# A depthwise convolution taken from VectorE to GpSimd (one half) and TensorE (the other half)

## The chip, the cores and the metric

The kernel runs on one core of a Trainium2 chip. The metric is the device time of one execution in microseconds (us). The kernel before takes 3819.85 us, the median of three runs from 3814.09 to 3823.12 us. The engines are named as in the profile: PE (TensorE, matrix products), PEld (its weight loads), DVE (VectorE), ACT (ScalarE), POOL (GpSimd) and SP (SyncE, which issues most of the transfers).

## What is computed

The whole network is a first block (attention, a state-space layer, a feed-forward layer with retrieved experts) and a second block of two layers. Each layer of the second block is feed-forward, mixer, feed-forward, on 512 tokens of width 1024. The mixer projects the tokens once, gives the parts to four sub-mixers, and projects the joined result back:

```
z = rmsnorm(x, mix_norm) @ w_in
(aq, ak, av, iq, ik, iw, bq, bk, bv, bg, br, cu, dcq, dckv, dkpe) = split(z)
y_a = dsa_mixer(aq, ak, av, iq, ik, iw, ...)     # attention over keys chosen by an index score
y_b = gla_mixer(bq, bk, bv, bg, br, ...)         # gated linear attention
y_c = conv_mixer(cu, c_dw_w, c_dw_b, c_norm)
y_d = mla_mixer(dcq, dckv, dkpe, ...)            # attention from latents
x = x + concatenate([y_a, y_b, y_c, y_d]) @ w_out

def conv_mixer(u, w_dw, b_dw, g_norm):
    a, gate = split(u, 2)
    h = a * sigmoid(gate)
    h = depthwise_conv(h, w_dw, padding=[(30, 0)]) + b_dw   # 31 taps, each of 256 channels by itself
    return silu(rmsnorm(h, g_norm))
```

The change concerns the depthwise convolution alone: 256 channels, 31 taps, 512 tokens. With channels on the 128 partitions these are two chunks of 128 x 512 numbers. Each of the 31 taps adds the input, shifted by the tap's number of tokens and multiplied by one number per channel.

## The kernel before

The feature dimension lies on the partitions and the 512 tokens along the free dimension. A projection block `proj(b)` makes 128 output features. Its weight (128x1024, `wr`) comes in by DMA. It is split into a high part `wh` by ACT (L1009) and a low part `wl` = `wr` - `wh` (L1010), on POOL for most of the mixer's blocks and on DVE for a few. 24 products of 128x512 follow on PE (L195 to L197: high by high, high by low, low by high, for 8 chunks). `wr`, `wh` and `wl` have two buffers each, so a weight is prepared at most two blocks ahead. The products accumulate in PSUM, and DVE evacuates them with the norm factor (L1066).

The mixer is a list of named steps (`ORDER`) that is issued in that order. A list scheduler with priorities then fixes one static order of instructions per engine. Each engine runs its own list in order, and a wait at the head of a list holds all that is behind it. The steps in the neighbourhood of the change are `hp` (the four projection blocks of the convolution, gated into the tile `hp`, `conv_in`), `ik`, `t3` and `iq` (blocks for the index score), `index` (the index score: PE L1234, ACT L1236, then DVE L1239/L1241), `lat` (three blocks for the latent attention, lat0 to lat2 below), and `conv`. `index` runs interleaved with `lat`. `conv` is 62 instructions on DVE: per chunk one TENSOR_SCALAR that also adds the bias (L1539) and 30 SCALAR_TENSOR_TENSOR that multiply and add (L1541). Far behind them stand `mla` (the latent attention), `qkn`, `rg` and `silu` (gates; L1120 also works on the convolution's result), and the four pieces `dsa0` to `dsa3`, before the output projection `wo`.

Of the kernel before, what the change touches and what calls it, by code (L numbers as in the profile page):

```python
# [9 lines left out]
F32 = mybir.dt.float32  # L10
# [3 lines left out]
AF = mybir.ActivationFunctionType  # L14
OP = mybir.AluOpType
# [4 lines left out]
P = 128  # L20
D = 1024
NCH = 8
T = 512
# [789 lines left out]
TAGS = {"x": 16, "ml": 12, "ds": 7, "sm": 4, "sd": 4, "gl": 10, "r": 2, "t3": 1, "rg": 2, "cv": 2, "rs": 1}  # L813
F_GRP = ((0, 8), (8, 15), (15, 22))
SWAP = np.r_[16:32, 0:16]
ORDER = "hp ik t3 iq exp index lat mla_in conv bqk v3 gla_in v2 v0 gla mla0 v1 mla1 mla3 qk mla2 qkn conv_norm topk2 rg silu topk1 y4 y2 topk3 y6 dsa0 dsa3 dsa1 dsa2".split()
WOP = ((0, 4, 2), (4, 8, 2))
YORD = (4, 5, 2, 3, 6, 7, 0, 1)

# [86 lines left out]
class Block2:  # L906
# [143 lines left out]
    def mixer(self, l, x):  # L1050
        net, nc, w, p = self.net, self.nc, self.w, self.p
        V = nc.vector
        first = {b: self.lw(self.A["w2"][l, b], 1024) for b in (13, 15)}
        xh, xl, rx = self.scaled(x, "mix")

        def proj(b):
            wh, wl = (a.rearrange("p (c m) -> p c m", c=NCH)
                      for a in first.pop(b, None) or self.lw(self.A["w2"][l, b], 1024, nc.vector if b in (14, 16) else nc.gpsimd))
            ps = net.ps("pa", "win")
            for c in range(NCH):  # L1060
                net.mm3(ps, (wh[:, c], wl[:, c]), (xh[c], xl[c]), c == 0, c == NCH - 1)
            return ps

        def keep(b, tag):
            t = self.mt(tag)
            V.tensor_mul(t, proj(b), rx)  # L1066
            return t

        def rsc():
            return self.mt("r")  # L1070

        def glsc():
            return self.mt("gl")
# [26 lines left out]
        def gla():  # L1100
            with net.banks("pd", "gla", glsc):
                v["gla"] = self.gla(v["glain"], *v["bqk"], vt)

        def mla(j):
            if "ya" not in v:
                v["ya"] = p.tile([P, 2, T + 30], F32, tag="hp", name=net.nm("ya"))[:, :, :T]
            with net.banks("pb", "mla"):
                self.mla(j, v["mla"], v["ya"])

        def qkn():  # L1110
            with net.banks("pc", "qkn", rsc):
                v["rq"] = self.qk_norm(v["qk"])

        def conv_norm():
            with net.banks("pd", "convn", rsc):
                self.conv_norm(v["acc"])

        def silu():
            for t in v["rg"] + v["acc"]:
                self.tc.keep_in_program_order(nc.scalar.activation(t, t, AF.Silu))  # L1120
            self.exp_set()

        def ysplit(c):
            for m in range(2):
                k = c + m
                yh[k], yl[k] = self.mt("x", F32R), self.mt("x", F32R)
                if c == 4:
                    src = v["acc"][m]
                elif c == 2:
                    src = v["gla"][m]  # L1130
                    V.tensor_mul(src, src, v["rg"][m])
                else:
                    src = v["ya"][:, m]
                net.split(src, yh[k], yl[k])

        def dsa(j):
            for c in range(2):
                if yh[c] is None:
                    yh[c], yl[c] = self.mt("x", F32R), self.mt("x", F32R)
            with net.banks(("pb", "pc")[j % 2], "dsa"):  # L1140
                self.dsa(j, v["masks"][j], v["qk"], v["rq"], vt, yh, yl, ("sm", "sd")[j % 2])

        steps = {
            "hp": lambda: v.update(hp=self.conv_in(proj, rx)),
            "exp": self.exp_set,
            "t3": lambda: v.update(t3=keep(3, "t3")),
            "iq": lambda: v.update(iq=[keep(0, "ds"), keep(1, "ds")]),
            "ik": lambda: v.update(ik=keep(2, "ds")),
            "index": index,
            "lat": lambda: v.update(lat=[keep(b, "ml") for b in (10, 11, 12)]),  # L1150
            "mla_in": mla_in,
            "bqk": lambda: v.update(bqk=[keep(8, "gl"), keep(9, "gl")]),
            "gla_in": gla_in,
            "conv": lambda: v.update(acc=self.conv(l, v["hp"])),
            "qk": lambda: v.update(qk=[keep(b, "ds") for b in (4, 5, 6, 7)]),
            "qkn": qkn,
            "gla": gla,
            "rg": lambda: v.update(rg=[keep(17, "rg"), keep(18, "rg")]),
            "conv_norm": conv_norm,
            "silu": silu,  # L1160
        }
        for j in range(4):
            steps[f"v{j}"] = lambda j=j: values(j)
            steps[f"mla{j}"] = lambda j=j: mla(j)
            steps[f"dsa{j}"] = lambda j=j: dsa(j)
            steps[f"topk{j}"] = lambda j=j: self.topk(v["masks"][j])
        for c in (2, 4, 6):
            steps[f"y{c}"] = lambda c=c: ysplit(c)
        for s in ORDER:
            steps[s]()  # L1170

        for a, e, g in WOP:
            for m0 in range(0, NCH, g):
# [39 lines left out]
    def index(self, iq, ik, t3):  # L1213

        net, nc, w, p = self.net, self.nc, self.w, self.p
        V = nc.vector
        iw = w.tile([P, 4, 8], F32, tag="iw", name=net.nm("iw"))
        ps = net.ps()
        for i in range(4):
            nc.tensor.transpose(ps[:, i * 8:(i + 1) * 8], t3[32:40, i * P:(i + 1) * P], net.c("ident")[32:40, 32:40])  # L1220
# [2 lines left out]
        for j in (3, 2, 1):  # L1223
            n = (j + 1) * P
            ts = slice(j * P, n)
            acc = self.mt("ds")[:, :n]
            for h in range(8):
# [5 lines left out]
                ps = net.ps()  # L1233
# [158 lines left out]
    def mla(self, j, qkv, ya):  # L1392
# [6 lines left out]
        for h in range(4):  # L1399
# [3 lines left out]
            if j:  # L1403
                nc.scalar.activation(sm[h][:, :j * P], ps[:, :j * P], AF.Identity, scale=r)
            V.scalar_tensor_tensor(sm[h][:, ts], ps[:, ts], r, self.caus, op0=OP.mult, op1=OP.add)
        self.softmax_pv(sm, n, lambda k, h: kv[k][:, 256 + h * 64:256 + (h + 1) * 64],
                        lambda c, po: nc.scalar.activation(ya[:, c, ts], po, AF.Copy))

    def gla_in(self, l, bq, bk, t3):
        net, nc, w, p = self.net, self.nc, self.w, self.p  # L1410
# [105 lines left out]
            out.append(o)  # L1516
        return out

    def conv_in(self, proj, rx):
        net, nc, w, p = self.net, self.nc, self.w, self.p  # L1520
        hp = p.tile([P, 2, T + 30], F32, tag="hp", name=net.nm("hp"))
        nc.gpsimd.memset(hp[:, :, :30], 0.0)
        for m in range(2):
            pa, pg = proj(13 + m), proj(15 + m)
            sg = net.sc(w)
            nc.vector.tensor_mul(hp[:, m, 30:], pa, rx)
            nc.vector.tensor_mul(sg, pg, rx)
            nc.scalar.activation(sg, sg, AF.Sigmoid)
            nc.vector.tensor_mul(hp[:, m, 30:], hp[:, m, 30:], sg)
        return hp  # L1530

    def conv(self, l, hp):
        net, nc, w = self.net, self.nc, self.w
        V = nc.vector
        dw = w.tile([P, 2, 31], F32, tag="dw", name=net.nm("dw"), bufs=1)
        nc.scalar.dma_start(dw.rearrange("p a b -> p (a b)"), self.A["dw"][l])
        acc = self.mts("cv", 2, F32)
        for m, a in enumerate(acc):
            V.tensor_scalar(a, hp[:, m, 0:T], dw[:, m, 0:1], self.gv("cb", m), op0=OP.mult, op1=OP.add)  # L1539
            for k in range(1, 31):  # L1540
                V.scalar_tensor_tensor(a, hp[:, m, k:k + T], dw[:, m, k:k + 1], a, op0=OP.mult, op1=OP.add)  # L1541
        return acc

    def conv_norm(self, acc):
        net, w = self.net, self.w
# [393 lines left out]
```

## Time and profile before

| | |
|---|---|
| median of three runs | 3819.85 us |
| the profiled execution | 3817.53 us, of which its span is 3815.8 us |
| PE busy | 3638.3 us (95%), 17229 instructions |
| DVE busy | 2584.0 us (68%) |
| ACT busy | 1444.5 us (38%) |
| POOL busy | 1087.8 us (29%), 693 instructions |
| the mixer of layer 0 | about 2065 to 2372 us |
| the mixer of layer 1 | about 3130 to 3442 us |

The span is the part of an execution that the profile covers. Busy times are of one execution, over very unlike stages: the first block takes up to about 1690 us, the two layers of the second block the rest. In a row of the timeline the first number is the start in microseconds from the start of the span, the second the length from the first start to the last end of the instructions merged in the row, and in brackets stands how long the engine was idle before it and whose end released it. The two mixers are built alike and only one of them needs to be read closely.

### The profile page before, as it was taken

How to read it: one execution, taken by the hardware profiler on the slowest of the kernel's cores; microseconds unless marked ns; L12 is line 12 of the kernel's file. 1: busy time of each engine (PE TensorE's matmuls, PEld its weight loads, DVE VectorE, ACT ScalarE, POOL GpSimd, SP SyncE). 2: the span in 40 equal slices, each digit the busy share in tenths (PEclk: the TensorE clock that was granted, in tenths of full speed). 3: DMA queues.
4: the chain of work that ended last, by engine and by line, in shares of the span. 5: the costliest groups of instructions: out<-in, count | busy, mean ns of one | idle time of the engine just before them, and what ended most of it. 6: DMA issues, size and time to landing. Idle time of an engine off the chain costs nothing.

```text
span 3815.8 us, 46368 instructions
## 1 busy us (share of the span) xinstructions
PE 3638.3 (95%) x17229; PEld 2975.1 (78%) x17229; DVE 2584.0 (68%) x4684; ACT 1444.5 (38%) x2401; POOL 1087.8 (29%) x693
## 2 busy tenths in 40 slices
PE   7798989989999999989999899999999998999999
PEld 6656877878988988878887577788788875667887
DVE  8668988788888888844445987434444459874343
ACT  3253369623333333342223446322322234463222
POOL 4424767455555555530001222000100013210000
PEclk8899989999999999999999999999999999999999
DMA  4212224788888888832222111222222221112223
GB/s 118 77 39 98 75 99 178 270 305 304 285 312 293 300 293 293 301 102 94 94 97 91 53 45 56 94 94 94 94 94 93 95 91 61 45 47 92 94 94 99
DMA packets 182081, 529.89 MB, mean 139 GB/s; under 512 B 22112, under 2 KB 73888, under 8 KB 163680
## 3 DMA queue, kind: packets, MB, share of 16 engines
q1 hardware_dynamic: 157840, 389.36, 30.6%
q0 software_dynamic: 18944, 134.75, 9.6%
q10 hardware_dynamic: 5072, 2.81, 0.3%
q8 instruction: 136, 2.23, 0.2%
q14 instruction: 89, 0.73, 0.1%
HBM read 495.51 MB, written 30.18 MB: 138 GB/s over the span
## 4 chain that ended last, share of the span: by engine, by line
PE 69%; DVE 8%; ACT 3%; DMA 3%; issue 2%; POOL 1%; ACTq 0%; POOLq 0%; DVEq 0%
PE ps L195 13%; PE ps L197 13%; PE ps L196 13%; PE V L1815 11%; PE S L197 3%; PE S L196 3%; PE S L195 3%; DVE cv L1541 2%; PE G L1749 2%; ACT gst L1750 1%; PE win L195 1%; PE win L197 1%; PE win L196 1%; DVE ds L1241 1%; DMA vr<-in_uv_dram 1%
## 5 line engine op out<-in xcount | busy, mean ns | idle before, releaser
L1009 ACT ACTIVATE wh<-wr 128x1024 fp32r<-128x1024 f32 (+1 forms) x334 | 347.4, 1040 | 1056.5 <-PE ps L196 759.4
L197 PE MATMUL ps<-x,wl 128*128 128x512 f32 x1408 | 557.0, 396 | 0.0
L195 PE MATMUL ps<-x,wh 128*128 128x512 f32 x1408 | 556.7, 396 | 0.0
L196 PE MATMUL ps<-x,wh 128*128 128x512 f32 x1408 | 556.6, 395 | 0.0
L989 POOL TENSOR_TENSOR s<-s,s 128x512 f32<-128x512 f32 x42 | 66.7, 1588 | 1161.6 <-ACT s L987 1150.4
L1806 POOL TENSOR_TENSOR vl<-vr,vh 128x1024 fp32r<-128x1024 f32 x128 | 324.2, 2533 | 177.8 <-ACT vh L1805 168.0
L1010 DVE TENSOR_TENSOR wl<-wr,wh 128x1024 fp32r<-128x1024 f32 (+1 forms) x288 | 343.9, 1194 | 43.8 <-ACT wh L1009 37.1
L197 PE MATMUL S<-pxh,ul 128*128 128x384 f32 x1024 | 349.7, 341 | 7.6 <-POOL ul L1767 7.6
L195 PE MATMUL S<-pxh,uh 128*128 128x384 f32 x1024 | 349.3, 341 | 0.0
L196 PE MATMUL S<-pxl,uh 128*128 128x384 f32 x1024 | 348.4, 340 | 0.0
L195 PEld LDWEIGHTS ps<-x,wh 128*128 128x128 f32 x1408 | 265.8, 189 | 63.9 <-ACT ml L947 1.1
L197 PEld LDWEIGHTS ps<-x,wl 128*128 128x128 f32 x1408 | 265.7, 189 | 62.7 <-issue 0.7
L196 PEld LDWEIGHTS ps<-x,wh 128*128 128x128 f32 x1408 | 265.8, 189 | 62.2 <-issue 0.5
L1815 PE MATMUL V<-vl,ah 128*128 128x512 f32 x768 | 303.5, 395 | 9.7 <-POOL vl L1806 9.7
L1815 PE MATMUL V<-vh,ah 128*128 128x512 f32 x768 | 300.7, 392 | 5.0 <-ACT vh L1805 2.6
L1815 PE MATMUL V<-vh,al 128*128 128x512 f32 x768 | 304.1, 396 | 0.9 <-DVE al L181 0.8
L195 PE MATMUL ps<-ml,wh 128*128 128x512 f32 x704 | 277.8, 395 | 0.0
L197 PE MATMUL ps<-ml,wl 128*128 128x512 f32 x704 | 277.8, 395 | 0.0
L1035 DVE TENSOR_TENSOR s<-ps,rs 128x512 f32<-128x512 f32 x88 | 60.9, 692 | 304.7 <-PE ps L197 304.7
L1876 POOL DMA_INDIRECT rows<-in_uv_dram,gidx x128 | 189.7, 1482 | 256.6 <-DVE acc L1885 225.7
L1047 DVE SCALAR_TENSOR_TENSOR hT<-ps,hT 128x512 f32<-128x512 f32 x96 | 66.4, 692 | 268.5 <-PE ps L197 268.5
L1767 DVE TENSOR_TENSOR ul<-ur,uh 128x1024 fp32r<-128x1024 f32 x100 | 184.8, 1848 | 65.8 <-ACT uh L1765 64.6
(578 smaller groups left out, 7997.4 us busy)
## 6 DMA issues: line engine op xcount, KB each, us to landing
wr<-in_f_gu_dram SPq DMA_DIRECT2D x176, 512.0 KB
ur<-in_ut_dram SPq DMA_DIRECT2D x128, 512.0 KB
vr<-in_uv_dram SPq DMA_DIRECT2D x128, 512.0 KB
wr<-in_f_dn_dram SPq DMA_DIRECT2D x64, 448.0 KB
gates<-gst SPq DMA_DIRECT2D x12, 2048.0 KB
gt<-gates SPq DMA_DIRECT2D x32, 768.0 KB
wr<-in_w_dram SPq DMA_DIRECT2D x46, 512.0 KB
wr<-in_f_dn_dram SPq DMA_DIRECT2D x32, 512.0 KB
```

The source lines that it names most:

```text
L195: mm(out, wh, xh, start=start, stop=False)
L196: mm(out, wh, xl, start=False, stop=False)
L197: mm(out, wl, xh, start=False, stop=stop)
L989: nc.gpsimd.tensor_tensor(sq, acc, sq, op=OP.add)
L1009: nc.scalar.activation(hi, raw, AF.Copy)
L1010: (eng or nc.vector).tensor_tensor(lo, raw, hi.bitcast(F32), op=OP.subtract)
L1541: V.scalar_tensor_tensor(a, hp[:, m, k:k + T], dw[:, m, k:k + 1], a, op0=OP.mult, op1=OP.add)
L1749: nc.tensor.matmul(ps[:, (t - t4) * P:(t - t4 + 1) * P], b, a, start=True, stop=True)
L1767: e.tensor_tensor(ul, raw, uh.bitcast(F32), op=OP.subtract)
L1806: nc.gpsimd.tensor_tensor(vl, raw, vh.bitcast(F32), op=OP.subtract)
L1815: nc.tensor.matmul(ps[k], x[:, ts], y[:, cs], start=b == 0 and n == 0, stop=b == P - 1 and n == 2)
L1876: nc.gpsimd.indirect_dma_start(r, None, self.A["uv"], bass.IndirectOffsetOnAxis(ap=self.gi[:, s:s + 1], axis=0))
```

## The change

Chunk 0 (`conv0`, a new step after `mla2`) becomes 31 products on PE, each of a 128x128 diagonal matrix with the input shifted by the tap. The matrix of each tap is made by one ACT instruction (the identity, scaled per partition) in one of four slots. The products are in plain float32 and accumulate in one PSUM bank; ACT then adds the bias.

Chunk 1 (`conv1`, in the place of the old step `conv`) becomes 61 instructions on POOL: per tap a TENSOR_SCALAR into a scratch tile and a TENSOR_TENSOR that adds it, except for the first tap, which needs only one. They are issued with their priority number raised by 1500, which makes the scheduler prefer other work of that engine.

Around this, `hp` is split into a tile for each chunk, and chunk 1 is projected first (blocks 14 and 16, and then 13 and 15, which are subtracted on DVE). The taps' numbers (`dw`) are loaded at the step `hp`, the two halves of the latent attention's result `ya` have tiles of their own, and the small tile `iw` has one buffer. Lines from about 1054 on stand some 13 to 28 lines further down in the kernel after the change (L1234 before is L1248 after).

```diff
-... qk mla2 qkn conv_norm topk2 rg silu ...
+... qk mla2 conv0 qkn conv_norm topk2 rg silu ...
...
-        first = {b: self.lw(self.A["w2"][l, b], 1024) for b in (13, 15)}
+        first = {b: self.lw(self.A["w2"][l, b], 1024) for b in (14, 16)}
...
-                      for a in first.pop(b, None) or self.lw(self.A["w2"][l, b], 1024, nc.vector if b in (14, 16) else nc.gpsimd))
+                      for a in first.pop(b, None) or self.lw(self.A["w2"][l, b], 1024, nc.vector if b in (13, 15) else nc.gpsimd))
...
+        def conv():
+            h0, h1, dw = v["hp"]
+
+            now = self.tc.cur_priority
+            self.tc.cur_priority = now + 1500
+            v["acc"] = [None, self.conv1(h1, dw)]
+            self.tc.cur_priority = now
+
+        def conv0():
+            h0, h1, dw = v["hp"]
+            with net.banks("pd", "conv"):
+                v["acc"][0] = self.conv0(h0, dw)
...
-        acc = self.mts("cv", 2, F32)
-        for m, a in enumerate(acc):
-            V.tensor_scalar(a, hp[:, m, 0:T], dw[:, m, 0:1], self.gv("cb", m), op0=OP.mult, op1=OP.add)
-            for k in range(1, 31):
-                V.scalar_tensor_tensor(a, hp[:, m, k:k + T], dw[:, m, k:k + 1], a, op0=OP.mult, op1=OP.add)
-        return acc
+    def conv1(self, hp, dw):
+
+        G = self.nc.gpsimd
+        t, a = self.mts("cv", 2, F32)
+        G.tensor_scalar(a, hp[:, 0:T], dw[:, 1, 0:1], self.gv("cb", 1), op0=OP.mult, op1=OP.add)
+        for k in range(1, 31):
+            G.tensor_scalar(t, hp[:, k:k + T], dw[:, 1, k:k + 1], None, op0=OP.mult)
+            G.tensor_tensor(a, a, t, op=OP.add)
+        return a
+
+    def conv0(self, hp, dw):
+
+        net, nc = self.net, self.nc
+        ps = net.ps()
+        dg = self.mt("sd").rearrange("p (a k) -> p a k", a=4)
+        for k in range(31):
+            nc.scalar.activation(dg[:, k % 4], net.c("ident"), AF.Identity, scale=dw[:, 0, k:k + 1])
+            nc.tensor.matmul(ps, dg[:, k % 4], hp[:, k:k + T], start=k == 0, stop=k == 30)
+        a = self.mt("cv")
+        nc.scalar.activation(a, ps, AF.Identity, bias=self.gv("cb", 0))
+        return a
```

On POOL the first place is layer 0, right behind the feed-forward layer's last additions (L989). Before, the subtractions of the weights for `ik`, `t3`, `iq` (two) and `lat` (the first) follow each other; `wl` is the low part that PE's block of that name waits for.

```order
L989 TENSOR_TENSOR s_17530<-s_17527,s_17530 128x512
L1010 TENSOR_TENSOR wl_17667<-wr_17665,wh_17666 128x1024
L1010 TENSOR_TENSOR wl_17700<-wr_17698,wh_17699 128x1024
L1010 TENSOR_TENSOR wl_17733<-wr_17731,wh_17732 128x1024
L1010 TENSOR_TENSOR wl_17766<-wr_17764,wh_17765 128x1024
L1010 TENSOR_TENSOR wl_17957<-wr_17955,wh_17956 128x1024
```

After, in the same place, `cv_18299` is the sum of chunk 1 and `cv_18298` the scratch tile.

```order
L989 TENSOR_TENSOR s_17530<-s_17527,s_17530 128x512
L1554 TENSOR_SCALAR cv_18299<-hp_17542,dw_17540,vec_2991_15099 128x512
L1556 TENSOR_SCALAR cv_18298<-hp_17542,dw_17540 128x512
L1557 TENSOR_TENSOR cv_18299<-cv_18299,cv_18298 128x512
L1556 TENSOR_SCALAR cv_18298<-hp_17542,dw_17540 128x512
L1557 TENSOR_TENSOR cv_18299<-cv_18299,cv_18298 128x512
L1556 TENSOR_SCALAR cv_18298<-hp_17542,dw_17540 128x512
L1010 TENSOR_TENSOR wl_17671<-wr_17669,wh_17670 128x1024
L1557 TENSOR_TENSOR cv_18299<-cv_18299,cv_18298 128x512
L1556 TENSOR_SCALAR cv_18298<-hp_17542,dw_17540 128x512
L1557 TENSOR_TENSOR cv_18299<-cv_18299,cv_18298 128x512
L1556 TENSOR_SCALAR cv_18298<-hp_17542,dw_17540 128x512
```

Six instructions of the convolution now stand ahead of the subtraction for `ik`. In the same way 9 stand between it and the one for `t3`, then 9, 8, 9 and 9 ahead of those for `iq`, `iq`, lat0 and lat1, and 11 ahead of lat2's, among them three smaller subtractions (`sm`, `sm`, `sd`). All 61 are ahead of lat2's subtraction, and layer 1 is the same.

On PE the place is behind the last block of the step `qk` (its last product is the `win` row, the projections' name). Before, `qkn` and the blocks of `rg` follow it.

```order
L197 MATMUL win_19092<-x_17485,wl_19088 128x512
L1266 MATMUL qkn_19193<-cst,r_19194 128x2 x4
L1266 MATMUL qkn_19193<-cst,r_19200 128x2 x4
L195 MATMUL win_19299<-x_17478,wh_19294 128x512
L196 MATMUL win_19299<-x_17486,wh_19294 128x512
```

After, the convolution's products (L1567, with the diagonal matrices in `sd_19196`) are there, between those of the latent attention.

```order
L197 MATMUL win_19094<-x_17485,wl_19090 128x512
L1567 MATMUL conv_19195<-hp_17599,sd_19196 128x512 x3
L1216 MATMUL mla_18937<-cst,sm_18905 128x128 x4
L1216 MATMUL mla_18945<-cst,sm_18906 128x128 x4
L1567 MATMUL conv_19195<-hp_17599,sd_19196 128x512
L1223 MATMUL mla_18952<-pt_18942,ml_18122 64x128
```

The 31 products stand in this neighbourhood, the last 16 of them in one piece behind the latent attention's last, and `qkn` and the blocks of `rg` come behind them. The products of the latent attention's values, which stood between the last block of `rg` and the output projection before, are ahead of `rg` now.

## Rows read from the trace of the kernel before

**Rows 1.** The page, part 1: busy time, share of the span and instructions.

```profile
PE 3638.3 (95%) x17229; PEld 2975.1 (78%) x17229; DVE 2584.0 (68%) x4684; ACT 1444.5 (38%) x2401; POOL 1087.8 (29%) x693
```

**Rows 2.** Windows: start:end, length, PE, PEld, DVE, ACT, POOL, clock, DMA, GB/s.

```profile
1800.00:1850.00 50.00, 50.00 (x217) 40.55 (x216) 18.22 (x21) 11.23 (x12) 0.00 (x0) 1.00 0.30 95
2101.00:2161.00 60.00, 48.17 (x176) 30.83 (x175) 60.00 (x82) 27.81 (x60) 19.42 (x8) 1.00 0.18 59
2161.00:2359.00 198.00, 189.99 (x981) 137.26 (x980) 167.99 (x419) 104.83 (x233) 36.95 (x16) 0.96 0.14 46
2213.10:2216.50 3.40, 3.40 (x10) 2.63 (x9) 3.40 (x8) 1.75 (x3) 0.00 (x0) 0.52 0.04 16
3130.00:3442.00 312.00, 291.51 (x1383) 211.19 (x1382) 268.60 (x537) 154.19 (x322) 72.54 (x32) 0.97 0.17 54
```

**Rows 3.** Groups of DVE in layer 0's mixer: busy us, mean ns, idle before.

```profile
L1541 DVE SCALAR_TENSOR_TENSOR cv<-hp,dw,cv 128x512 f32<-128x512 f32 x60 | 56.3, 966 | 0.3
```

**Rows 4.** Timeline of POOL, the weight subtractions of layer 0's mixer.

```profile
2085.99 2.65 POOL L1010 TENSOR_TENSOR wl<-wr,wh 128x1024 fp32r<-128x1024 f32 x1 [16.11 <-ACT wh L1009]
...
2139.50 1.54 POOL L1010 TENSOR_TENSOR sd<-wr,sd 128x512 fp32r<-128x512 f32 x1 [3.85 <-ACT sd L1009]
2145.85 2.54 POOL L1010 TENSOR_TENSOR wl<-wr,wh 128x1024 fp32r<-128x1024 f32 x1 [4.82 <-ACT wh L1009]
```

**Rows 5.** Timeline of DVE: the gated input of the first chunk.

```profile
2082.26 0.69 DVE L1529 TENSOR_TENSOR hp<-hp,s 128x512 f32<-128x512 f32 x1 [0.72 <-ACT s L1528]
```

**Rows 6.** Timeline of PE where lat2's block starts and ends.

```profile
2155.64 0.40 PE L195 MATMUL win<-x,wh 128*128 128x512 f32 x1
...
2161.22 1.88 PE L229 MATMUL mlain<-s,cst 128*128 128x512 f32 x4
...
2163.17 0.39 PE L196 MATMUL win<-x,wh 128*128 128x512 f32 x1
```

**Rows 7.** Groups of POOL by form in the whole span; busy us, mean ns.

```profile
L1748 POOL TENSOR_SCALAR gb<-cst,iT 128x128 f32<-128x128 f32 x144 | 98.9, 693 | 54.3 <-PE G L1749 45.4 <-DVE ga L1745 4.2 <-DVE gb L1748 3.6
...
L989 POOL TENSOR_TENSOR s<-s,s 128x512 f32<-128x512 f32 x42 | 66.7, 1588 | 1161.6 <-ACT s L987 1150.4 <-issue 9.8 <-POOL s L989 1.0
...
L282 POOL TENSOR_TENSOR wl<-wr,wh 128x512 fp32r<-128x512 f32 x10 | 12.9, 1294 | 49.4 <-ACT wh L281 49.4
...
L1731 POOL TENSOR_SCALAR nT<-gT 128x128 f32<-128x128 f32 x4 | 2.1, 532 | 13.4 <-ACT gT L1724 13.4
...
L1646 POOL TENSOR_SCALAR rxf<-rxf 128x64 f32<-128x64 f32 x4 | 1.5, 376 | 0.4
```

**Rows 8.** Line L1748 by itself: ns min/median/max, on either engine.

```profile
L1748 DVE TENSOR_SCALAR gb<-cst,iT x240: 270/286/1835, 527.9 to 708.1; 128x128 f32<-128x128 f32 x120
L1748 POOL TENSOR_SCALAR gb<-cst,iT x144: 594/659/1587, 528.1 to 707.3; 128x128 f32<-128x128 f32 x144
```

**Rows 9.** Timeline of POOL in the first block, a chain of additions and products.

```profile
57.69 2.34 POOL L529 TENSOR_TENSOR Q<-Q,Q 128x1024 f32<-128x1024 f32 x1
60.10 1.98 POOL L527 TENSOR_TENSOR Q<-bc,dn 128x1024 f32<-128x1024 f32 x1
```

**Rows 10.** Timeline of DVE in the same stretch, two-input instructions.

```profile
57.81 2.26 DVE L391 TENSOR_TENSOR cm<-un 128x32 f32<-128x32 f32 x1
60.11 0.19 DVE L392 TENSOR_TENSOR sst<-sst,cm 128x32 f32<-128x32 f32 x1
```

**Rows 11.** Groups of DVE between 2101 and 2161 us.

```profile
L1541 DVE SCALAR_TENSOR_TENSOR cv<-hp,dw,cv 128x512 f32<-128x512 f32 x48 | 43.2, 935 | 0.0
```

**Rows 12.** Groups of ACT between 2161 and 2372 us.

```profile
L1407 ACT ACTIVATE ya<-mla 128x128 f32<-128x128 f32 x8 | 2.2, 278 | 5.2 <-PE mla L1209 5.2
```

**Rows 13.** Timeline of PE behind a wait of 1.82 us.

```profile
2212.66 0.66 PE L1445 MATMUL gla<-cst,gl 128*128 128x128 f32 x4 [1.82 <-DVE gl L1442]
```

**Rows 14.** Timeline from the last block of `rg` to the output projection.

```profile
2305.45 0.40 PE L197 MATMUL win<-x,wl 128*128 128x512 f32 x1
...
2315.65 1.65 PE L195 MATMUL wo<-x,wh 128*128 128x512 f32 x3
```

More of the change, by code (lines that the diff above doesn't have):

```diff
@@ L815 @@
 SWAP = np.r_[16:32, 0:16]
-ORDER = "hp ik t3 iq exp index lat mla_in conv bqk v3 gla_in v2 v0 gla mla0 v1 mla1 mla3 qk mla2 qkn conv_norm topk2 rg silu topk1 y4 y2 topk3 y6 dsa0 dsa3 dsa1 dsa2".split()
+ORDER = "hp ik t3 iq exp index lat mla_in conv bqk v3 gla_in v2 v0 gla mla0 v1 mla1 mla3 qk mla2 conv0 qkn conv_norm topk2 rg silu topk1 y4 y2 topk3 y6 dsa0 dsa3 dsa1 dsa2".split()
 WOP = ((0, 4, 2), (4, 8, 2))
@@ L1105, in mla @@
             if "ya" not in v:
-                v["ya"] = p.tile([P, 2, T + 30], F32, tag="hp", name=net.nm("ya"))[:, :, :T]
+                v["ya"] = [p.tile([P, T + 30], F32, tag="hp1", name=net.nm("ya"))[:, :T], p.tile([P, T], F32, tag="ya", name=net.nm("ya"))]
             with net.banks("pb", "mla"):
@@ L1132, in ysplit @@
                 else:
-                    src = v["ya"][:, m]
+                    src = v["ya"][m]
                 net.split(src, yh[k], yl[k])
@@ L1143, in mixer @@
         steps = {
-            "hp": lambda: v.update(hp=self.conv_in(proj, rx)),
+            "hp": lambda: v.update(hp=self.conv_in(l, proj, rx)),
             "exp": self.exp_set,
@@ L1153, in mixer @@
             "gla_in": gla_in,
-            "conv": lambda: v.update(acc=self.conv(l, v["hp"])),
+            "conv": conv,
+            "conv0": conv0,
             "qk": lambda: v.update(qk=[keep(b, "ds") for b in (4, 5, 6, 7)]),
@@ L1216, in index @@
         V = nc.vector
-        iw = w.tile([P, 4, 8], F32, tag="iw", name=net.nm("iw"))
+        iw = w.tile([P, 4, 8], F32, tag="iw", name=net.nm("iw"), bufs=1)
         ps = net.ps()
@@ L1406, in mla @@
         self.softmax_pv(sm, n, lambda k, h: kv[k][:, 256 + h * 64:256 + (h + 1) * 64],
-                        lambda c, po: nc.scalar.activation(ya[:, c, ts], po, AF.Copy))
+                        lambda c, po: nc.scalar.activation(ya[c][:, ts], po, AF.Copy))
     def gla_in(self, l, bq, bk, t3):
@@ L1517, in gla, with conv_in @@
         return out
-    def conv_in(self, proj, rx):
+    def conv_in(self, l, proj, rx):
         net, nc, w, p = self.net, self.nc, self.w, self.p
-        hp = p.tile([P, 2, T + 30], F32, tag="hp", name=net.nm("hp"))
-        nc.gpsimd.memset(hp[:, :, :30], 0.0)
-        for m in range(2):
+        dw = w.tile([P, 2, 31], F32, tag="dw", name=net.nm("dw"), bufs=1)
+        nc.scalar.dma_start(dw.rearrange("p a b -> p (a b)"), self.A["dw"][l])
+        hp = []
+        for m in (1, 0):
+            h = p.tile([P, T + 30], F32, tag=f"hp{m}", name=net.nm("hp"))
+            nc.gpsimd.memset(h[:, :30], 0.0)
@@ L1524, in conv_in @@
             pa, pg = proj(13 + m), proj(15 + m)
             sg = net.sc(w)
-            nc.vector.tensor_mul(hp[:, m, 30:], pa, rx)
+            nc.vector.tensor_mul(h[:, 30:], pa, rx)
             nc.vector.tensor_mul(sg, pg, rx)
             nc.scalar.activation(sg, sg, AF.Sigmoid)
[L1529 to L1536, printed above, removed]
-        acc = self.mts("cv", 2, F32)
-        for m, a in enumerate(acc):
-            V.tensor_scalar(a, hp[:, m, 0:T], dw[:, m, 0:1], self.gv("cb", m), op0=OP.mult, op1=OP.add)
-            for k in range(1, 31):
-                V.scalar_tensor_tensor(a, hp[:, m, k:k + T], dw[:, m, k:k + 1], a, op0=OP.mult, op1=OP.add)
-        return acc
+            nc.vector.tensor_mul(h[:, 30:], h[:, 30:], sg)
@@ new lines, in conv_in @@
+            hp.append(h)
+        return hp[1], hp[0], dw
+    def conv1(self, hp, dw):
[16 more added lines that the diff above has]
+        return a
```

## Prediction

> **What bounds the kernel now.** I read the page's busy shares first: PE is busy 95% of the span, with DVE at 68% and POOL at 29% [rows 1]. That says that work added to PE costs its length nearly everywhere, and that POOL has room on average. It is an average over unlike stages, so the windows come next [rows 2]. In a feed-forward stretch PE is busy 50.00 of 50 us; the change has nothing there. The mixer falls in two. From 2101 to 2161 us it is DVE that is busy 60.00 of 60 us, and 48 of the convolution's instructions take 43.2 us of that [rows 11]; PE is modelled busy 48.17 us, but its weight loads take 30.83 us against 40.55 in a dense 50, so dense work would need about 30.83 x 50 / 40.55 = 38 us. I call this phase 1; it ends where lat2's block starts on PE. From 2161 to 2359 us PE is busy 189.99 of 198 us: phase 2 is bound by PE. Layer 1's mixer has the same shares (291.51 of 312 us on PE, 268.60 on DVE), so I work one layer out and double it.
>
> Then POOL's timeline [rows 4]: its weight subtractions take 2.4 to 2.65 us and come just in time, the one for `ik` at 2085.99 and the one for lat2 at 2145.85, ending at 2148.4, 7 us before PE starts lat2 at 2155.64 [rows 6]. A block is 24 products in (2161.22 - 2155.64) = 5.6 us. So POOL is idle for most of the time, but PE cannot take a block before POOL's subtraction for it, and only two blocks' weights fit ahead.
>
> **What leaves.** DVE loses 60 instructions of 56.3 us in all, and the two that begin a chunk [rows 3]. In phase 1 this frees the bounding engine. Whether that shortens anything depends on what is late next, and that is the subtractions.
>
> **What POOL gets.** The order of after puts all 61 instructions of conv1 among the subtractions of phase 1, ahead of lat2's. A raised priority number does not help once the static order stands: POOL takes its list in order. Chunk 1's input is ready at 2082.26 + 0.69 = 2082.95 [rows 5], and from there on POOL has one chain to the end of lat2's subtraction:
>
> - 31 TENSOR_SCALAR of 128x512. The trace has none of this size on POOL. Rows of 64 and 128 columns take 376 and 532 ns [rows 7], 2.44 ns a column; 384 columns more than 128 give 0.53 + 0.94 = 1.47 us. The lower end is 0.53 us (no quicker than 128 columns); the upper one starts from the form with a number per partition, mean 693 ns at 128 columns [rows 7]: 1.63 us. I take 1.50, nearest to the sloped rows: 46.5 us.
> - 30 TENSOR_TENSOR of 128x512: 1294 ns where POOL is nearly alone, 1588 ns at L989 beside DVE's work [rows 7]. I take 1.40: 42.0 us.
> - 61 gaps between dependent instructions: 60.10 - (57.69 + 2.34) = 0.07 us [rows 9], 4.3 us.
> - seven subtractions (`ik`, `t3`, two `iq`, three `lat`) at 2.6 us, 18.2 us, and three smaller at 1.54 us, 4.6 us [rows 4].
>
> Sum 115.6 us, so lat2's weight is ready at 2198.6 instead of being in time at 2155.64: **+43 us**. Seen block by block: 9 instructions of about 1.5 us and a subtraction of 2.6 make 16 us between weights, for a block that PE does in 5.6, so PE will wait some 10 us per block. DVE's relief does not count against it: it ends in the same wait. Nothing else of PE's list can fill the gaps, since the list is fixed and conv0's products stand far behind. Behind a block that waits stand the index score's products and all of phase 2.
>
> The Trainium skill, GPSIMD Engine Reference, section 4.1 (Engine selection), says that GpSimd is about two times slower than VectorE on two-input instructions but "1-input is roughly line-rate". By that a TENSOR_SCALAR here would be far below 1.5 us. The trace speaks against it at 128 columns: the same line takes 286 ns on DVE and 659 ns on POOL in the median [rows 8]. What it would make of the sum is the first rival.
>
> **What PE gets.** 31 float32 products of 128x512 in phase 2. Two such products (four records) and one ordinary product lie between 2161.22 and 2163.17 [rows 6]: 1.95 - 0.23 = 1.72 us, 0.86 us each, so **+26.7 us**. PE is the bound there, with at most 198 - 189.99 = 8.0 us of waits to fill. The bounds are 18.7 us (all waits filled) and 31 (clock low for a few microseconds).
>
> **What ACT gets.** 31 instructions of 128x128 at 0.28 us [rows 12], 8.7 us, and one evacuation. ACT is busy 104.83 of 198 us in phase 2 [rows 2], four slots hold matrices ahead, and 0.28 us is under PE's 0.86: nothing. Without this cover it would be 8.7 us.
>
> **What moves.** The latent attention's last products lay between the last block of `rg` (2305.45) and `wo` (2315.65) [rows 14]. Those 10.2 us are the gates' way through DVE and ACT, and the products covered part of it. They now stand ahead of `rg`, and only the other attention's products remain. Bounds 0 and +10; I take +5. PE's clock: behind a wait of 1.82 us [rows 13] the granted clock is 0.52 for 3.4 us, the 1.2 GHz level [rows 2], which loses about 1.6 us. Behind PE's new waits in phase 1 this is inside POOL's chain; only lat2's block pays, +2. Of the 8.0 us of waits in phase 2 a part disappears as DVE is free of what was left of the convolution: -4. The swap of the first two blocks, the split tiles and the earlier load of the taps leave the number of subtractions and of bytes as it was; at nothing, under the feed-forward's dense PE work; if it shows, 1 to 2 us.
>
> **Sum.** Per layer 42.9 + 26.7 + 5 + 2 - 4 = 72.6 us, twice 145 us. On the profiled execution of 3817.5 us this gives 3963 us; the median of the runs stands 2.3 us above it, so 3965 us.
>
> **Rivals.**
>
> Quick one-input instructions on POOL: each TENSOR_SCALAR at its lower end of 0.53 us takes 31 x 0.97 = 30 us out of the chain. +43 becomes +13, a layer +42.6, the time 3817.5 + 85 + 2.3 = 3905 us. For it: nothing in the trace has 512 columns. Against it: time grows with the columns in three rows, and POOL is 2.3 times slower than DVE on the same line.
>
> Ports: POOL's two-input work and DVE's hold each other up. In the first block a DVE instruction of 128x32 that takes 0.19 us takes 2.26 us beside a POOL instruction of 2.34 us [rows 9, 10]. The Trainium skill, SBUF — State Buffer, tells of this pair as an exclusive lock for the whole instruction, and these rows agree. DVE itself has room for waits, being rid of 43 of 60 us, but POOL may wait in its turn: the 24 two-input instructions of the index score at about 0.7 us are 17 us (60.00 - 43.2 [rows 2, 11]), and POOL's own at the upper ends (1.63 and 1.588) 4 + 6 us. A layer +100, the time about 4019 us.
>
> The other side, not slower: if POOL kept ahead, phase 1 would fall from DVE's 60 us to PE's 38, phase 2 would fill its 8 us, and 26.7 us would be added: 26.7 - 22 - 8 = -3 us a layer, 3813 us in all, no difference that can be told. This decides if a weight comes every 5.6 us, that is nine instructions in 5.6 - 2.6 = 3.0 us, 0.33 us each. For it: POOL's 29% and DVE's full 60 us. Against it: the least two-input row is four times that.
>
> That the change does not do what it says (conv1 behind the weights in truth): the order of after shows it ahead of them, and the order is fixed.
>
> **Chances.** The forecast 0.62 (its own range 3935 to 3995); quick instructions 0.13; ports 0.17; not slower 0.03; that phase 2 or the gates make up more than I allow, 0.05. A range from 3895 to 4020 holds the first three but for the far ends of both. About 0.2% (7.6 us) is what a measurement of this kernel can tell from no change: faster 0.03, within it 0.02, slower 0.95.
>
> **What would show it.** On POOL, rows of L1556 near 1.5 us and of L1557 near 1.4 us, and lat2's subtraction ending near 2200. On PE, waits for `wl` of about 10 us per block between 2090 and 2200, released by POOL; 31 products of L1567 at 0.86 us apart; phase 2 as dense as before. On DVE, idle time in phase 1. It is wrong if PE's blocks in phase 1 follow each other as before (then the durations on POOL are off), or if PE waits there for DVE or ACT instead.

## The result and the profile after

The changed kernel takes 3994.26 us in the median of four runs (3988.9 to 3995.54), the kernel before beside it 3816.97 us: a ratio of 1.0456, 95% interval 1.0442 to 1.047. It is 177 us slower. The forecast was 145 us slower, 3965 us, with a range from 3895 to 4020; the narrower range that it called its own, 3935 to 3995, holds the result by 1 us. The profiled execution has a span of 3991.5 us, 175.7 us more than before.

The first part of the page, against [rows 1]: POOL has 170 us more and PE 84 us more, DVE 89 us less.

```profile
PE 3722.0 (93%) x17353; PEld 3010.1 (75%) x17353; DVE 2495.2 (63%) x4560; ACT 1469.1 (37%) x2465; POOL 1257.6 (32%) x817
```

I cut each mixer at three points of PE's timeline: its first projection product, the first product behind lat2 (`mlain`, L229), and the first product of `wo`. Phase 1 lies between the first two, phase 2 between the last two. The windows of layer 0, first of the kernel before, then of the changed one (columns as in [rows 2]):

```profile
2065.80:2161.20 95.40, 82.35 (x319) 57.77 (x318) 85.00 (x106) 40.33 (x74) 28.87 (x12) 1.00 0.20 66
2161.20:2315.70 154.50, 146.56 (x754) 106.75 (x752) 138.39 (x345) 80.49 (x166) 31.91 (x13) 0.96 0.15 48
```

```profile
2064.80:2215.50 150.70, 94.70 (x320) 65.88 (x319) 49.79 (x89) 40.61 (x74) 112.46 (x73) 0.80 0.13 42
2215.50:2397.60 182.10, 171.38 (x816) 117.63 (x814) 131.73 (x307) 93.03 (x204) 34.11 (x14) 0.97 0.12 40
```

Phase 1 is 55.3 us longer, and in it PE is idle for 56 us of 150.7 where it was idle for 13 of 95.4. Its mean granted clock falls to 0.80: behind the waits PE runs for some microseconds at the lower of its two levels (1.2 GHz), with products 0.43 us apart instead of 0.23. Phase 2 is 27.6 us longer and nearly as dense as before: PE is idle for 10.7 us of it instead of 7.9. Layer 1 gives +55.0 and +28.7 us in the same way. Together that is 167 us; some 8 us more lie in the feed-forward layers between the two mixers (741 us before, 749 after). Of these one wait makes 4 us. It stands ahead of the first product of layer 1's mixer, where before that product came first:

```profile
3214.80 1.35 PE L992 MATMUL ps<-s,cst 128*128 128x512 f32 x2 [4.00 <-POOL s L989]
```

POOL's timeline of the changed kernel in layer 0 answers to [rows 4]:

```profile
2082.13 0.77 POOL L1554 TENSOR_SCALAR cv<-hp,dw,vec 128x512 f32<-128x512 f32 x1 [13.21 <-DVE hp L1546]
2082.87 1.57 POOL L1556 TENSOR_SCALAR cv<-hp,dw 128x512 f32<-128x512 f32 x1
2084.53 1.29 POOL L1557 TENSOR_TENSOR cv<-cv,cv 128x512 f32<-128x512 f32 x1
...
2090.49 2.34 POOL L1010 TENSOR_TENSOR wl<-wr,wh 128x1024 fp32r<-128x1024 f32 x1
...
2106.55 2.34 POOL L1010 TENSOR_TENSOR wl<-wr,wh 128x1024 fp32r<-128x1024 f32 x1
...
2169.16 2.34 POOL L1010 TENSOR_TENSOR wl<-wr,wh 128x1024 fp32r<-128x1024 f32 x1
...
2195.02 1.27 POOL L1010 TENSOR_TENSOR sd<-wr,sd 128x512 fp32r<-128x512 f32 x1 [3.57 <-ACT sd L1009]
2205.45 2.41 POOL L1010 TENSOR_TENSOR wl<-wr,wh 128x1024 fp32r<-128x1024 f32 x1 [9.15 <-ACT wh L1009]
```

POOL is one chain without a gap from 2082 to 2191.5, where the convolution and two of the three small subtractions are done; then it waits for ACT twice. The weights for `ik` and `t3` come 16 us apart where they came 5.5 us apart, and lat2's, the last row, is ready at 2207.9. PE's timeline shows who waits, and under it stand the sums of the waits in phase 1 (us in total, times, longest):

```profile
2108.94 0.80 PE L197 MATMUL win<-x,wl 128*128 128x512 f32 x1 [8.80 <-POOL wl L1010]
2124.87 0.79 PE L197 MATMUL win<-x,wl 128*128 128x512 f32 x1 [8.18 <-POOL wl L1010]
...
2175.45 5.06 PE L1248 MATMUL index<-ds,qb 128*128 128x512 f32 x6 [21.55 <-ACT r L1250]
...
2187.35 5.70 PE L1248 MATMUL index<-ds,qb 128*128 128x384 f32 x10 [4.63 <-ACT r L1250]
...
2204.30 0.39 PE L195 MATMUL win<-x,wh 128*128 128x512 f32 x1
...
2209.89 0.39 PE L195 MATMUL win<-x,wh 128*128 128x512 f32 x1
...
2210.36 0.39 PE L197 MATMUL win<-x,wl 128*128 128x512 f32 x1
...
2215.49 1.88 PE L229 MATMUL mlain<-s,cst 128*128 128x512 f32 x4
```

```profile
PE index L1248 <- ACT r L1250: 29.0, 6, 21.6
PE win L197 <- POOL wl L1010: 25.7, 4, 8.8
```

Four waits for `wl` sum to 25.7 us and those of the index score for ACT to 29.0 us, 54.7 us together. The four are those of `ik`, `t3` and the two of `iq`. Lat1's and lat2's blocks start at 2204.30 and 2209.89 and run without a wait: PE comes to them late, and lat2's first product with `wl` runs at 2210.36, 2.5 us after that weight was ready. The long wait of the index score was not in the forecast. The timeline of SP and ACT tells where it comes from:

```profile
2171.52 12.55 SPq L1008 DMA_DIRECT2D wr<-in_uq_dram  x2
2174.28 0.63 ACT L1009 ACTIVATE sm<-wr 128x512 fp32r<-128x512 f32 x1 [21.47 <-DMA wr<-in_uq_dram]
2174.81 0.58 ACT L1250 ACTIVATE r<-index 128x512 f32<-128x512 f32 x1
```

POOL's subtraction for lat1 (2169.16 to 2171.5) gives a `wr` buffer free; only then does SP load the next weight, and ACT's split of it (L1009) stands in ACT's list ahead of the index score's next step (L1250). So one late subtraction on POOL stops ACT, and through ACT the products on PE: the index score's and lat0's, which are interleaved with them. The splits of the two other small weights do the same behind it, with waits of 4.63 and 1.87 us. The stretch from the end of the long wait to the end of phase 1 in the changed kernel is the second of these windows; the first holds the same products in the kernel before:

```profile
2129.54:2161.22 31.68, 28.20 (x106) 18.82 (x106) 31.68 (x45) 15.98 (x36) 9.36 (x5) 1.00 0.18 56
2175.45:2215.49 40.04, 33.03 (x106) 21.51 (x107) 30.48 (x70) 16.44 (x37) 21.47 (x14) 0.84 0.15 47
```

So 47 of the 55 us are lost up to 2175.45, and 8 behind it, 3.5 of them in waits and 4.8 in products at a lower granted clock.

The convolution's products in phase 2, the longest piece of them (32 records are 16 products):

```profile
2357.82 14.01 PE L1567 MATMUL conv<-hp,sd 128*128 128x512 f32 x32
2371.66 1.51 PE L1280 MATMUL qkn<-cst,r 128*128 128x2 f32 x13
```

(2371.66 - 2357.82) / 16 = 0.865 us a product, against the 0.86 us worked out from [rows 6].

### The profile page after: what moved, and what is told of

The parts are those of the page before. It is cut to its first block, busy times and chain, and to the rows that moved or that the text cites. A ratio compares the mean times of both kernels' runs of the same rounds, so it can differ in the third digit from the quotient of the medians.

```text
span 3991.5 us, 46728 instructions
## 1 busy us (share of the span) xinstructions
PE 3722.0 (93%) x17353; PEld 3010.1 (75%) x17353; DVE 2495.2 (63%) x4560; ACT 1469.1 (37%) x2465; POOL 1257.6 (32%) x817
## 4 chain that ended last, share of the span: by engine, by line
PE 69%; POOL 7%; DVE 5%; ACT 2%; issue 2%; DMA 1%; SPq 0%; POOLq 0%; ACTq 0%; DVEq 0%
PE ps L197 12%; PE ps L196 12%; PE ps L195 12%; PE V L1843 11%; PE S L196 3%; PE S L197 3%; PE S L195 3%; POOL cv L1556 2%; PE G L1777 2%; POOL cv L1557 2%; PE conv L1567 1%; PE win L195 1%; PE win L197 1%; PE win L196 1%; ACT gst L1778 1%
## 5 line engine op out<-in xcount | busy, mean ns | idle before, releaser
L1009 ACT ACTIVATE wh<-wr 128x1024 fp32r<-128x1024 f32 (+1 forms) x334 | 347.3, 1040 | 1160.2 <-PE ps L196 742.9
L989 POOL TENSOR_TENSOR s<-s,s 128x512 f32<-128x512 f32 x42 | 67.4, 1605 | 1152.4 <-ACT s L987 1141.1
```

Of the source, the lines that this page charges most:

```text
L1009: nc.scalar.activation(hi, raw, AF.Copy)
```

## The experiments

The theory is that two things add up, the chain on POOL ahead of the weights and the products on PE. The rivals are that one of them is the whole cost, and that POOL's and DVE's instructions hold each other up (the rival "ports"). Each time below stands with the ratio to the kernel before that ran beside it, since that kernel itself took from 3813.8 to 3826.6 us in the median of these occasions. Phase lengths are those of layer 0.

**Only POOL.** Chunk 0 goes back to DVE, and the step `conv0` goes; buffers of `cv` and `ya` are changed to fit.

```diff
-            dg ... nc.tensor.matmul(ps, dg[:, k % 4], hp[:, k:k + T], ...)
+            V.scalar_tensor_tensor(a, hp[:, k:k + T], dw[:, 0, k:k + 1], a, op0=OP.mult, op1=OP.add)
```

> Chunk 1 on GpSimd as in the changed kernel, chunk 0 back on VectorE as before; no convolution on TensorE. Theory (the loss is two separate things, GpSimd's chain ahead of the weights, about 54 us a layer, and the 31 products on TensorE, about 27 us a layer): lat2's block ends as late as in the changed kernel, the part behind it is as long as before: 3817 + 2 x 57 = 3930 us (3915 to 3945). Rival (the products and their matrices on TensorE are the main cost and GpSimd's chain is mostly hidden): under 3870 us.

Measured: 3930.45 us, ratio 1.0304 (1.0287 to 1.0321). Phase 1 is 156.7 us, phase 2 149.5. The time is the one forecast: with chunk 0 on DVE, POOL's chain costs about 60 us a layer, and phase 2 without the products is 5 us shorter than before.

**Only PE.** Chunk 1 goes back to DVE, without the raised priority number.

```diff
-            G.tensor_scalar(t, hp[:, k:k + T], dw[:, 1, k:k + 1], None, op0=OP.mult)
-            G.tensor_tensor(a, a, t, op=OP.add)
+            V.scalar_tensor_tensor(a, hp[:, k:k + T], dw[:, 1, k:k + 1], a, op0=OP.mult, op1=OP.add)
```

> Chunk 1 back on VectorE, chunk 0 on TensorE as in the changed kernel; no convolution on GpSimd. Theory: the weights come in time again, VectorE has half of the convolution, so the part up to lat2's block shrinks by some 13 us against the kernel before, and the part behind it grows by 27 us: 3817 + 2 x 15 = 3847 us (3830 to 3865). Rival (products are the main cost): 3900 us or more.

Measured: 3875.72 us, 1.0155 (1.0138 to 1.0172), between both expectations. The windows of its two phases:

```profile
2067.70:2158.80 91.10, 83.00 (x319) 57.46 (x318) 75.51 (x120) 40.45 (x74) 25.70 (x12) 1.00 0.21 71
2158.80:2342.90 184.10, 173.42 (x815) 119.12 (x813) 131.27 (x306) 93.42 (x204) 34.15 (x14) 0.96 0.12 39
```

Phase 2 has the 28 us and more, as expected. Phase 1 gains 4 us and not 13, although DVE is idle for 16 of 91 us now: PE's own work fills 83. The feed-forward layers between the mixers are 5 us longer here too, and are not in the kernel with POOL alone. The wait of 4.0 us at L992 stands in every kernel here with conv0 on PE, and in none with chunk 0 on DVE. So that small cost comes with conv0 on PE.

**Without the scaling.** The 30 scaling instructions are left out, so chunk 1 is not the convolution.

```diff
-            G.tensor_scalar(t, hp[:, k:k + T], dw[:, 1, k:k + 1], None, op0=OP.mult)
-            G.tensor_tensor(a, a, t, op=OP.add)
+            G.tensor_tensor(a, a, hp[:, k:k + T], op=OP.add)
```

> As the changed kernel, but chunk 1's 30 scaling instructions on GpSimd are left out (30 unscaled additions stay). Theory: GpSimd's chain up to lat2's weight is 30 x (1.56 + 0.08) = 49 us shorter, and the time follows nearly one for one: 3994 - 2 x 47 = 3900 us (3888 to 3912). Rival (the part up to lat2 is held by the shared ports of VectorE and GpSimd, to which scaling instructions with one input contribute nothing): 3970 us or more.

Measured: 3908.05 us, 1.0248 (1.0231 to 1.0265). Phase 1 falls from 150.7 to 110.7 us for 49 us less on POOL. It follows POOL's chain, except for 9 us: the waits for `wl` still sum to 19.2 us, but those of the index score only to 1.2, and in the last 30.1 us of phase 1 PE's own work is the bound (29.2 us busy).

**Subtractions of phase 1 on DVE.**

```diff
-... nc.vector if b in (13, 15) else nc.gpsimd
+... nc.vector if b in (13, 15, 2, 3, 0, 1, 10, 11, 12) else nc.gpsimd    # and both of mla_in's weights
```

> As the changed kernel, but the ten weight subtractions between the convolution's blocks and the end of lat2 are on VectorE, so that no weight stands behind the convolution in GpSimd's list. Theory: TensorE no longer waits for weights there; with VectorE free of the convolution that part ends earlier than before the change (by 10 to 20 us), the part behind it is 28 us longer: 3817 + 2 x 12 = 3840 us (3815 to 3860). Rival (ports: GpSimd's additions hold VectorE's subtractions and the index score up): 3880 us or more.

Measured: 3927.94 us, 1.0299 (1.0282 to 1.0316): the total lies where the rival had it, but not for its reason. Phase 1 is 89.6 us, less than before the change; phase 2 is 211.5. On PE and POOL one finds

```profile
2184.74 0.79 PE L197 MATMUL win<-x,wl 128*128 128x512 f32 x1 [29.19 <-POOL wl L1010]
```

```profile
2181.13 1.26 POOL L1557 TENSOR_TENSOR cv<-cv,cv 128x512 f32<-128x512 f32 x1
2182.34 4.66 POOL L1010 TENSOR_TENSOR wl<-wr,wh 128x1024 fp32r<-128x1024 f32 x2
```

The first weight left on POOL is that of the block behind lat2, and all 61 instructions still stand ahead of it. The wait moved to it.

**All subtractions on DVE.** Every block of the mixer.

```diff
-... nc.vector if b in (13, 15) else nc.gpsimd
+... nc.vector                                                            # and both of mla_in's weights
```

> As the changed kernel, but all weight subtractions of the projection blocks and of the latent attention's weights are on VectorE: GpSimd has only the convolution's 61 instructions in the mixer. Theory: the 29 us wait that the kernel with ten subtractions moved had for the first block behind lat2 goes too; the part up to lat2 is some 5 us shorter than before the change, the part behind it 28 us longer: 3817 + 2 x 25 = 3867 us (3855 to 3885). Rival (ports: 61 instructions on GpSimd beside VectorE's two-input work cost time themselves): 3900 us or more.

Measured: 3875.59 us, 1.0128 (1.0111 to 1.0145). Phase 1 is 89.6 us, phase 2 189.0 (182.1 in layer 1). Now PE waits for no weight, and what is left is about the price of conv0 on PE: the kernel with PE alone stands at 1.0155. So conv1 on POOL costs nothing where no weight stands behind it and DVE is free of the convolution. Why phase 2 of layer 0 is 7 us longer than in the changed kernel stays open.

**One tap on PE.** 30 diagonal matrices and products are left out, so chunk 0 is not the convolution.

```diff
-        for k in range(31):
+        for k in range(1):
```

> As the changed kernel, but chunk 0 has one tap on TensorE; 30 diagonal matrices and products of each layer are left out. Theory (the products add their full length of 0.87 us, since the part behind lat2's block is bound by TensorE): 3994 - 2 x 26 = 3942 us, a few microseconds less if the small delay seen in the feed-forward layers behind goes with them (3930 to 3948). Rival (they partly fill waits): 3960 us or more.

Measured: 3935.62 us, 1.0285 (1.0267 to 1.0302). Phase 2 is 152.9 and 156.5 us in the two layers against 182.1 and 181.9: 27.3 us in the mean for 30 products, 0.91 us each. The 8 us between the mixers stay (748 us), so they don't come from the number of products.

**A raw buffer of their own for two weights.**

```diff
+        if tag:
+            raw = w.tile([P, 512], F32, tag="wq", name=net.nm("wr"), bufs=1)[:, :n]
+        else:
             raw = w.tile([P, 1024], F32, tag="wr", name=net.nm("wr"), bufs=2)[:, :n]
```

> As the changed kernel, but the two weights of the latent attention's projections get a raw buffer of their own (512 columns, one buffer; the tag gl has 9 buffers instead of 10 to make room), so that ScalarE's split of them no longer waits for the transfer that lat1's subtraction on GpSimd releases. Theory (the index score's 21.6 us wait is this split at the head of ScalarE's list, and it makes the part up to lat2 54 us longer where GpSimd's chain alone gives 43): 10 us a layer come back, 3994 - 20 = 3974 us (3964 to 3982). Rival (GpSimd's chain alone sets that part, and the index score's wait lies beside it): 3990 us or more.

Measured: 3960.94 us, 1.0348 (1.0329 to 1.0367), against 1.0456 for the changed kernel; the gain is somewhat larger than the expected range. Phase 1 is 134.9 us, 15.8 less. The index score's waits for ACT sum to 6.1 us instead of 29.0, and now PE does wait for lat2's weight:

```profile
2193.18 0.80 PE L197 MATMUL win<-x,wl 128*128 128x512 f32 x1 [7.64 <-POOL wl L1013]
```

The edit also let the scheduler put the three small subtractions behind lat2's, which takes some 4 us out of POOL's chain by their lengths; the 12 us beyond these are then the ACT path.

**Taps in small groups.** Chunk 0 on DVE; chunk 1 on POOL, pinned behind single subtractions over both phases.

```diff
+TAPS = {2: 1, 3: 1, 1: 1, 10: 1, 11: 1, 12: 2, 8: 1, 9: 1, 22: 4, 21: 2, 19: 1, 20: 2, 4: 3, 5: 5, 6: 3, 7: 2}   # taps behind block b's weight
...
+            if b in TAPS:
+                self.taps(v["c1"], range(v["k"], v["k"] + TAPS[b]))
```

> Chunk 0 on VectorE as before; chunk 1 on GpSimd, but its taps are pinned in small groups behind single weight subtractions from ik to the last block of qk, as many as GpSimd was idle there before the change (the tag gl has 9 buffers to make room). Theory (what costs is the place in GpSimd's list, not the work there): no weight is late, the part up to lat2 is some 5 us shorter for VectorE's relief, the part behind it as before: 3815 - 2 x 5 = 3805 us (3795 to 3825). Rival (work on GpSimd costs wherever it stands, by ports or by weights): 3850 us or more.

Measured: 3869.12 us, 1.0112 (1.0095 to 1.0129). My expectation fell: PE never waits for `wl` now, and yet both phases are longer than before the change:

```profile
2070.20:2171.70 101.50, 85.42 (x320) 60.10 (x319) 77.26 (x109) 40.49 (x75) 47.54 (x25) 0.95 0.17 60
2171.70:2350.00 178.30, 155.76 (x739) 112.28 (x737) 142.24 (x309) 80.59 (x163) 103.43 (x62) 0.89 0.11 39
```

PE has many waits of 1 to 6 us for DVE and ACT, and the granted clock is 0.89 in phase 2. That brought back the rival of the ports, and three kernels test it by itself: the kernel before, with unused work on POOL at these same places.

**Loads on POOL: scaling and addition, memsets, two scalings.**

```diff
+            keep(G.tensor_scalar(z, self.rope, 0.5, None, op0=OP.mult))   # load 1 and 3
+            keep(G.tensor_tensor(z, z, self.rope, op=OP.add))             # load 1
+            keep(G.memset(z, 0.0))                                        # load 2, six times
+            keep(G.tensor_scalar(z, z, 0.5, None, op0=OP.mult))           # load 3
```

> The kernel before, both chunks on VectorE, and beside it work on GpSimd that nobody uses: at the places of the last experiment 31 pairs of one scaling and one addition of 128x512 (the small tile iw has one buffer to make room). Theory A (ports: a GpSimd instruction that reads keeps VectorE's two-input instructions waiting and the other way round): VectorE, which bounds the part up to lat2, is held up; 40 to 120 us slower than before. Theory B (only the place in GpSimd's list counts, later weights): also slower, 20 to 60 us, and the same with work that reads nothing. If the taps fit as planned: within 10 us of before.

> As the load with scalings and additions, but in the place of each pair six memsets of 128x512, about as long (524 ns for one in the trace of before, 3.1 us for six) and reading nothing. Theory A (ports): within 15 us of before, clearly faster than the load that reads. Theory B (place in the list): as slow as the load that reads, within 15 us.

> As the load with scalings and additions, but two one-input scalings in the place of each pair (62 of about 1.56 us). Theory A1 (any GpSimd instruction that reads conflicts): as slow as the load with additions, within 15 us. Theory A2 (only GpSimd's two-input additions conflict): near the load of memsets. Theory B: all three alike.

Measured: 3865.52 us, 1.0131 (1.0113 to 1.015) for scaling and addition; 3817.67 us, 1.0005 (0.9995 to 1.0015) for memsets; 3838.32 us, 1.006 (1.0044 to 1.0077) for two scalings. The groups of layer 0's mixer, in this order; DVE's taps took 966 ns in the mean before [rows 3]:

```profile
L1550 DVE SCALAR_TENSOR_TENSOR cv<-hp,dw,cv 128x512 f32<-128x512 f32 x60 | 64.2, 1098 | 0.3
...
L1525 POOL TENSOR_SCALAR dm<-rope 128x512 f32<-128x512 f32 x31 | 52.1, 1682 | 1.3
L1526 POOL TENSOR_TENSOR dm<-dm,rope 128x512 f32<-128x512 f32 x31 | 42.7, 1376 | 2.6
```

```profile
L1526 POOL MEMSET dm<- 128x512 f32 x186 | 99.1, 533 | 9.7
...
L1550 DVE SCALAR_TENSOR_TENSOR cv<-hp,dw,cv 128x512 f32<-128x512 f32 x60 | 58.2, 998 | 0.3
```

```profile
L1550 DVE SCALAR_TENSOR_TENSOR cv<-hp,dw,cv 128x512 f32<-128x512 f32 x60 | 60.5, 1037 | 0.3
...
L1525 POOL TENSOR_SCALAR dm<-rope 128x512 f32<-128x512 f32 x31 | 52.3, 1687 | 1.2
L1526 POOL TENSOR_SCALAR dm<-dm 128x512 f32<-128x512 f32 x31 | 49.3, 1589 | 2.6
```

99 us of memsets a layer cost nothing that can be measured; 95 us of reading work cost 50 us in two layers, and 102 us of one-input work 23 us. So neither A1 nor A2 holds alone: both kinds that read hold DVE up, additions more. The single taps on DVE show it. Three rows of the kernel with scalings and additions are a tap with nothing beside it, an addition, and the tap that starts beside that addition:

```profile
2133.41 0.74 DVE L1550 SCALAR_TENSOR_TENSOR cv<-hp,dw,cv 128x512 f32<-128x512 f32 x1
...
2156.34 1.39 POOL L1526 TENSOR_TENSOR dm<-dm,rope 128x512 f32<-128x512 f32 x1
2156.51 1.76 DVE L1550 SCALAR_TENSOR_TENSOR cv<-hp,dw,cv 128x512 f32<-128x512 f32 x1
```

Over both layers, the 14 taps of this kernel that start beside an addition take 1.68 us in the mean and end 0.55 us behind it (the median). Those beside a scaling take 0.85 to 0.89 us in the mean and 1.10 at most, and the 46 beside a memset, in the kernel with memsets, take the 0.74 us of a tap alone. The taps beside a weight subtraction take up to 2.9 us, in the kernel before too, which is why its mean is 966 ns. Theory B is out for these places. Work on POOL that reads has a price of its own where DVE is busy, about 25 us a layer for this load, and that is about what the spread taps lost.

**A second operation in the scaling.** In the changed kernel L1554 takes 0.77 us and L1556 twice that for the same shape.

```diff
-            G.tensor_scalar(t, hp[:, k:k + T], dw[:, 1, k:k + 1], None, op0=OP.mult)
+            G.tensor_scalar(t, hp[:, k:k + T], dw[:, 1, k:k + 1], self.one[:, 0:1], op0=OP.mult, op1=OP.mult)
```

> As the changed kernel, but each of the 30 scalings has a second operation, a multiplication by a column of ones. In the trace of the changed kernel the one TENSOR_SCALAR with two operations (L1554, 128x512) takes 0.76 us and those with one operation (L1556) 1.56 us. Theory P (the form with two operations is the quicker one on GpSimd): L1556 falls to about 0.77 us, the chain up to lat2 is 30 x 0.8 = 24 us shorter a layer, the time 3994 - 2 x 24 = 3946 us (3935 to 3960). Theory Q (L1554 is quick for another reason, its unshifted input or the addition): L1556 stays at 1.5 us or more, no change from 3994 us.

Measured: 3948.48 us, 1.0341 (1.0324 to 1.0358). The line by itself, first in the changed kernel, then here (ns, least, median, most):

```profile
L1556 POOL TENSOR_SCALAR cv<-hp,dw x60: 1557/1563/1997, 2082.9 to 3336.9; 128x512 f32<-128x512 f32 x60
```

```profile
L1556 POOL TENSOR_SCALAR cv<-hp,dw,one x60: 767/768/1199, 2084.2 to 3291.3; 128x512 f32<-128x512 f32 x60
```

A second operation halves the instruction's time. Phase 1 is 128.4 us, 22.3 less, close to 30 x 0.8 = 24. It confirms once more that phase 1 follows POOL's chain. No version tried beats the kernel before.

## Why the forecast came out as it did

- The mechanism was right for the first four blocks: fixed order, the convolution ahead of the weights, PE waiting block by block. The kernels with POOL alone, without scaling and with the quicker scaling each show phase 1 following the chain. It was not right for the end of phase 1, where lat2's weight was to decide: it was ready at 2207.9, not 2198.6, and PE did not wait for it. The prediction named waits of PE for ACT in phase 1 as a sign of being wrong, and 29.0 of the 54.7 us of waits are of that kind. The size came out near because those waits too hang on POOL's chain.
- Durations on POOL: forecast 1.50 and 1.40 us, measured 1.60 and 1.30 in layer 0's means, so a pair came out at the forecast 2.90 us because two errors cancel, which is luck. The convolution ended at 2190, and the small subtraction behind it at 2191.5. With the last small one and lat2's directly behind, lat2's weight would have been ready at about 2195, an estimate from their lengths (1.27 and 2.41 us), against the forecast 2198.6.
- The term that was mis-sized is phase 1: 43 and 2 us for the clock forecast, 55 measured. Its weak step is "+43 us" as POOL's chain to lat2's weight: I counted what stands on POOL, and not that a subtraction also frees the raw buffer of the next weight, whose split stands on ACT ahead of the index score. The wait of 21.6 us delayed the index score and lat0's products, which are interleaved with it, to 2204.3; then both lat1's and lat2's blocks were still to come, where the forecast had one block. The lower clock behind the waits costs 4.8 us there instead of 2 (0.84 in the last 40 us). With the separate raw buffer phase 1 is 39.5 us longer than before, and lat2's weight is waited for as forecast.
- "+26.7 us" for the products: measured 0.865 us apart, 26.8 us, and phase 2 +27.6 and +28.7 against a forecast of 26.7 + 5 - 4 = 27.7. The products' term is shown by the kernel with one tap. The -4 was wrong: PE's idle time in phase 2 grew by 2.8 us in layer 0. How much the gates took of the +5 was not measured, so that the two nearly cancel is in part luck.
- The 8 us in the feed-forward layers were not in the sum. About 4 of them are PE's wait at L992, by a change of PE's fixed order that comes with conv0 on PE, whatever the number of its products. The cause of the rest stays open.
- The rival "not slower" took PE's need in phase 1 as 38 us of the 60 between 2101 and 2161. That was wrong: with weights in time and DVE relieved, phase 1 shrinks by 4 to 6 us, not by 22. PE was busy for 82 to 83 us of phase 1 in those kernels. That weight loads in proportion to a dense stretch underrate a stretch of short and single products is my reading of it and not tested.
- The rival "quick one-input instructions" was wrong for the form that the kernel uses, and right for a form beside it. The Trainium skill, GPSIMD Engine Reference, section 4.1 (Engine selection), says that "1-input is roughly line-rate". L1554 and the last experiment, 0.77 us for 512 columns, agree with that far better than the 1.56 us of the one-operation form; DVE takes 0.54 us for the same form (L1548 of the kernel with memsets). My 1.50 came from rows of this slower form.
- The rival "ports" has a part: the loads show a price of reading work on POOL. In the changed kernel DVE was idle for two thirds of phase 1, so I expect little of it there; it was not measured by itself.

## What to carry to other kernels

A low average share of an engine is no room if each of its few instructions is just in time: ask what stands behind the added work in its list, and then whose buffer, transfer and next engine wait for that. A raised priority number does not keep work late: here the scheduler put the raised instructions in between the weights, and the order that results is fixed. Moving work off the engine that bounds a stage gains only down to the next engine's need, so take that need from busy time, 83 of 95 us here, not from a ratio.

## What the runs showed of the hardware

- A TENSOR_SCALAR of 128x512 float32 on GpSimd, scaled by a number per partition, takes 1.56 us with one operation and 0.77 us with two.
- GpSimd's memsets (533 ns for 128x512) beside VectorE's work cost nothing, 1.0005 (0.9995 to 1.0015); instructions that read cost 0.6% (two scalings) to 1.3% (scaling and addition) of this kernel for about the same busy time.
- A two-input instruction of 0.74 us on VectorE takes 1.68 us in the mean when it starts beside a two-input addition on GpSimd, 0.85 to 0.89 us beside a one-operation TENSOR_SCALAR, and 0.74 us beside a memset.
